# One-hot tiles of the gate matrices laid out token by token, all made on VectorE, with six more score blocks in that stage

## The chip, the cores and the metric

The kernel runs on one core of a Trainium2 chip. The metric is the device time of one execution in microseconds; a smaller number is better. TensorE (PE) multiplies matrices into PSUM, VectorE (DVE), ScalarE (ACT) and GpSimd (POOL) do elementwise work, and SyncE (SP) issues most of the transfers. Every engine works through its own instructions in the order in which they stand, and waits for the others through semaphores.

## What is computed

Two transformer blocks on 512 tokens of width 1024. Each ends in a feed-forward layer of 16384 experts, of which every token takes 16 for each of 8 heads (128 in all). The part of the reference that the change touches, the same in both blocks:

```
s = einsum('thsd,hsnd->thsn', q, sub_keys)      # two halves of 128 keys
sv, si = top_k(s, 16)
cand = sv[:, :, 0, :, None] + sv[:, :, 1, None, :]
top, pos = top_k(cand, 16)                      # 16 experts per head
e = take_along_axis(cidx, pos)                  # expert numbers
g = softmax(top)                                # gates
act = gelu(einsum('thkd,td->thk', u_tab[e], xb))
out = einsum('thk,thkd->td', g * act, v_tab[e])
```

## The kernel before, in words

The function `peer` is called twice, once for each block's expert layer, and takes about half of the span. Its last 128 tokens (tile `TL`) gather their experts' rows from DRAM. For the other 384 tokens (`NDT`) nothing is gathered: the layer is computed densely over all 16384 experts, in 128 blocks of 128 experts. It has these stages.

1. **Routing** (`peer_route`) finds each token's 128 expert numbers `ei` and gates `GT`. Meanwhile PE makes the first 19 **score blocks**. A score block `e` is `gelu(U_e x)` for 128 experts and 384 tokens: a load of `ur`, a rounded part `uh` on ACT, the rest `ul` on POOL, 24 matmuls into `pa`, and a Gelu on ACT into the tile `ga`. At most `NA` = 28 finished blocks lie in SBUF.
2. **The gate stage** builds the dense gate matrix: for each token a 128 x 128 matrix G[e // 128, e % 128] with the gates of its 128 chosen experts. With p running over the token's 128 choices it is a matmul of two one-hot tiles: `oh2` (the low 7 bits of the number equal to the column) and `oh1` (the high 7 bits equal to the column, times the gate; itself the product of the small tiles `oha`, 8 wide, and `ohb`, 16 wide). The stage goes over 12 groups (`NTG`) of 32 tokens (`TG`). For every 8 tokens two instructions over 128 x 1024 elements make `oh2` (on VectorE, line 1199) and `oh1` (line 1201: on GpSimd, and each fourth on VectorE). PE multiplies token by token into `pgg`, four tokens to a PSUM tile, and ACT copies each into `stg` (line 1209). After 32 tokens `stg` goes to DRAM (`Gd`). In the tiles the token index runs fastest, so the 128 elements that PE reads for one token lie 8 elements (32 bytes) apart, in both operands. `run_ahead` puts score blocks between the groups: three ahead of the first group (`TB`), one after each group named in `RG` (3, 6, 9, 11), and two behind the stage, up to 28.
3. **The stream** runs over the 128 blocks. Item `e` reads its gates back (`gbuf`, four items to a load), forms `w` = gates x scores on VectorE, splits it and the rows of V into rounded part and rest (`wh`, `wl`, `vh`, `vl`), emits score block `e + 28`, and adds `w V` into the six PSUM tiles `y` with 18 matmuls. Beside it VectorE handles the gathered rows of the last tile (`urow`, `vrow`, gathered by POOL).

The order on VectorE and GpSimd in the stream is that of the code. Elsewhere a scheduler places instructions by priority, so that a block's matmuls can stand among those of the gate matrices.

Of the kernel before, what the change touches and what calls it, by code (L numbers as in the profile page):

```python
# [23 lines left out]
def build(tc, I, out, dbg=None, stop=None):  # L24
# [571 lines left out]
    for h in range(8):  # L596
# [14 lines left out]
        for t in range(NT):  # L611
# [142 lines left out]
    for h2 in range(2):  # L754
        if h2 == 1:
            ws = keep_w(wk, I["w_mem_o"], 8, 0)
        for t in range(NT):
# [3 lines left out]
            for hh in range(2):  # L761
# [10 lines left out]
                for j in range(2):  # L772
# [298 lines left out]
    def peer(keysT_d, U, UT, Vt, front, finish, nm, side=None, also=None, then=None):  # L1071
# [108 lines left out]
        irep = r1.tile([128, 128, 8], BF16, name="irep")  # L1180
        V.tensor_copy(out=irep, in_=iota.unsqueeze(2).broadcast_to([128, 128, 8]))
        irtg = r1.tile([128, 16, TG], BF16, name="irtg")
        V.tensor_copy(out=irtg, in_=iota[:, 0:16].unsqueeze(2).broadcast_to([128, 16, TG]))
        for tg in range(NTG):
            stg = rw.tile([128, 128, TG], F32, name="stg", tag="stg")

            def row(j, c0, n, m):
                return sT[j][:, c0:c0 + n].unsqueeze(1).broadcast_to([128, m, n])

            c0 = tg * TG  # L1190
            oa_ = rw.tile([128, 8, TG], F32, name="oha", tag="oha")
            V.tensor_tensor(out=oa_, in0=irtg[:, 0:8], in1=row(0, c0, TG, 8), op=OP.is_equal)
            V.tensor_tensor(out=oa_, in0=oa_, in1=row(3, c0, TG, 8), op=OP.mult)
            ob_ = rw.tile([128, 16, TG], F32, name="ohb", tag="ohb")
            V.tensor_tensor(out=ob_, in0=irtg, in1=row(1, c0, TG, 16), op=OP.is_equal)
            for t8 in range(TG // 8):
                tk = slice(t8 * 8, t8 * 8 + 8)
# [6 lines left out]
                for q in range(2):  # L1204
# [668 lines left out]
```

## Time and profile before

| | us |
|---|---|
| median of 3 executions | 4033.55 (4032.31 to 4042.46) |
| the profiled execution | 4039.25, of which the span is 4037.5 |
| PE busy | 3859.8 (96% of the span) |
| DVE busy | 3101.3 (77%) |
| POOL busy | 2146.8 (53%) |
| ACT busy | 1659.2 (41%) |
| mean granted clock of TensorE | 0.977 of full speed |

Shares over the whole span hide that the two expert layers differ from the rest: there one must look at each stage by itself, at which engine has no idle time in it and which engine the others wait for. The gate stage of the first layer runs from 753 to 954 us, that of the second from 2870 to 3070; each is followed by its stream.

### The profile page before, as it was taken

The numbers are of one execution on the slowest core, as the hardware profiler recorded it, in microseconds if no ns is written. First come the engines' busy times: TensorE is split into PE (matmuls) and PEld (weight loads), VectorE is DVE, ScalarE is ACT, GpSimd is POOL, SyncE is SP. The second block draws the span as 40 slices with busy tenths as digits, with TensorE's granted clock in tenths as the row PEclk, the third lists the DMA queues.
The fourth block names the chain that finished last, engine by engine and source line by source line (L and its number), as shares of the span: only waits on it lengthen the run. The fifth ranks groups of instructions, "written<-read, shape, count | busy, mean of one in ns | idle before, by whom it ended". The sixth has DMA issues, their size and how long they took to land. (4 is left out here: it accounts for less than half of the span.)

```text
span 4037.5 us, 53263 instructions
## 1 busy us (share of the span) xinstructions
PE 3859.8 (96%) x19062; PEld 3367.6 (83%) x19062; DVE 3101.3 (77%) x5460; ACT 1659.2 (41%) x2567; POOL 2146.8 (53%) x1333
## 2 busy tenths in 40 slices
PE   6999999899999999999899988999899999999999
PEld 5767788899899999987777766788899999999987
DVE  8456589884898888877756566689885898888875
ACT  3454432454333333333444567332454333333333
POOL 3000047654788887750424433257655778887750
PEclk8999999999999999999999989999999999999999
DMA  3333132235999889987222322332236999999884
GB/s 112 98 102 115 61 112 74 103 133 195 313 332 316 314 315 314 328 286 261 91 81 58 93 73 93 116 111 78 106 136 218 320 324 316 315 317 314 303 272 151
DMA packets 330057, 784.31 MB, mean 194 GB/s; under 512 B 32048, under 2 KB 148864, under 8 KB 326400
## 3 DMA queue, kind: packets, MB, share of 16 engines
q1 hardware_dynamic: 252608, 499.86, 37.6%
q0 software_dynamic: 77184, 281.05, 19.5%
q8 instruction: 150, 2.46, 0.2%
q14 instruction: 115, 0.94, 0.1%
HBM read 722.98 MB, written 56.65 MB: 193 GB/s over the span
## 5 line engine op out<-in xcount | busy, mean ns | idle before, releaser
L1106 POOL TENSOR_TENSOR ul<-ur,uh 128x1024 fp32r<-128x1024 f32 x256 | 713.7, 2788 | 263.9 <-ACT uh L1100 177.1
L1113 PE MATMUL pa<-phi,uh 128*128 128x384 f32 x2048 | 695.1, 339 | 0.6 <-ACT ga L1118 0.6
L1114 PE MATMUL pa<-plo,uh 128*128 128x384 f32 x2048 | 694.2, 339 | 0.0
L1300 PE MATMUL y<-vl,wh 128*128 128x512 f32 x1536 | 599.8, 392 | 5.7 <-DVE vl L1273 5.7
L1301 PE MATMUL y<-vh,wl 128*128 128x512 f32 x1536 | 601.8, 393 | 0.0
L1299 PE MATMUL y<-vh,wh 128*128 128x512 f32 x1536 | 595.6, 392 | 1.7 <-ACT vh L1272 1.6
L1273 DVE TENSOR_TENSOR vl<-vr,vh 128x1024 fp32r<-128x1024 f32 x256 | 341.4, 1334 | 216.1 <-ACT vh L1272 215.9
L1248 DVE SCALAR_TENSOR_TENSOR acc<-vrow,act,acc 128x1024 f32<-128x1024 f32 x256 | 423.6, 1655 | 50.0 <-DMA vrow<-in_expert_v_dram,ei 25.3
L1237 DVE SCALAR_TENSOR_TENSOR urow<-urow,hgat 128x1024 f32<-128x1024 f32 x256 | 416.5, 1634 | 28.9 <-DMA urow<-in_peer_u_dram,ei 17.4
L1271 ACT CAST wh<-w 128x384 fp32r<-128x384 f32 x256 | 131.4, 513 | 745.8 <-PE y L1300 607.0
L1116 PE MATMUL pa<-phi,ul 128*128 128x384 f32 x2048 | 403.9, 340 | 18.5 <-POOL ul L1106 18.4
L1100 ACT CAST uh<-ur 128x1024 fp32r<-128x1024 f32 x256 | 269.6, 1053 | 356.6 <-issue 233.4
L1113 PEld LDWEIGHTS pa<-phi,uh 128*128 128x128 f32 x2048 | 388.7, 190 | 9.8 <-ACT ga L1118 1.0
L1114 PEld LDWEIGHTS pa<-plo,uh 128*128 128x128 f32 x2048 | 388.8, 190 | 9.6
L1116 PEld LDWEIGHTS pa<-phi,ul 128*128 128x128 f32 x2048 | 362.9, 190 | 21.0 <-POOL ul L1106 21.0
L1207 PE MATMUL pgg<-oh,oh 128*128 128x128 f32 x1536 | 373.8, 421 | 4.8 <-DVE oh L1199 4.0
L1207 PEld LDWEIGHTS pgg<-oh,oh 128*128 128x128 f32 x1536 | 369.9, 337 | 7.2 <-issue 5.0
L1301 PEld LDWEIGHTS y<-vh,wl 128*128 128x128 f32 x1536 | 288.7, 188 | 65.8 <-DVE wl L1274 2.7
L1300 PEld LDWEIGHTS y<-vl,wh 128*128 128x128 f32 x1536 | 289.0, 188 | 64.6 <-DVE vl L1273 9.5
L1299 PEld LDWEIGHTS y<-vh,wh 128*128 128x128 f32 x1536 | 288.4, 188 | 57.4 <-ACT vh L1272 4.0
L77 DVE TENSOR_TENSOR wl<-wr,wh 128x512 fp32r<-128x512 f32 (+1 forms) x276 | 201.4, 738 | 146.9 <-ACT wh L76 146.8
L1270 DVE TENSOR_TENSOR w<-gbuf,ga 128x384 f32<-128x384 f32 x256 | 261.8, 1024 | 45.7 <-DMA ur<-in_expert_uT_dram 21.6
(538 smaller groups left out, 7662.9 us busy)
## 6 DMA issues: line engine op xcount, KB each, us to landing
vr<-in_peer_v_dram SPq DMA_DIRECT2D x128, 512.0 KB, 6.2
ur<-in_peer_uT_dram SPq DMA_DIRECT2D x128, 512.0 KB, 4.1
vr<-in_expert_v_dram SPq DMA_DIRECT2D x128, 512.0 KB, 6.7
ur<-in_expert_uT_dram SPq DMA_DIRECT2D x128, 512.0 KB, 4.3
gbuf<-Gd SPq DMA_DIRECT2D x64, 768.0 KB, 9.7
Gd<-stg SPq DMA_DIRECT2D x24, 1920.0 KB, 6.1
wr<-in_w_in_dram SPq DMA_DIRECT2D x104, 256.0 KB, 2.7
war<-in_w_ada_dram SPq DMA_DIRECT2D x24, 512.0 KB, 6.9
```

What stands on the lines that cost most here:

```text
L1100: A.copy(out=uh, in_=ua[e])
L1106: G.tensor_tensor(out=ul, in0=raw, in1=uh.bitcast(F32), op=OP.subtract)
L1113: T.matmul(pa, uh[:, k, :], hi[:, k, 0:NDT], start=(k == 0), stop=False)
L1114: T.matmul(pa, uh[:, k, :], lo[:, k, 0:NDT], start=False, stop=False)
L1116: T.matmul(pa, ul[:, k, :], hi[:, k, 0:NDT], start=False, stop=(k == 7))
L1207: T.matmul(pg[:, j, :], oh2[:, :, 4 * q + j], oh1[:, :, 4 * q + j], start=True, stop=True)
L1237: V.scalar_tensor_tensor(out=row, in0=row, scalar=1.0, in1=hg_, op0=OP.mult, op1=OP.mult, accum_out=act[:, k:k + 1])
L1248: V.scalar_tensor_tensor(out=acc, in0=rows_.pop((1, k)), scalar=act[:, k:k + 1], in1=acc, op0=OP.mult, op1=OP.add)
L1273: V.tensor_tensor(out=vl, in0=vr, in1=vh.bitcast(F32), op=OP.subtract)
L1299: T.matmul(y[t][c], wh[:, ts], vh[:, cs_], start=(e_ == 0), stop=False)
L1300: T.matmul(y[t][c], wh[:, ts], vl[:, cs_], start=False, stop=False)
L1301: T.matmul(y[t][c], wl[:, ts], vh[:, cs_], start=False, stop=(e_ == 127))
```

## The change

The one-hot tiles become token-major: `oh2` and `oh1` are [128, 8 tokens, 128] in place of [128, 128, 8 tokens], so that a token's 128 elements lie side by side. `oha` and `ohb` are turned in the same way. VectorE makes all of them; GpSimd has none left. The constant tiles `irep` and `irtg`, which repeated the column numbers, go; a broadcast view of a 128-wide `iob` takes their place, and the token's value is now the operand that is repeated along the inner dimension. `oh1` has two buffers in place of three.

`run_ahead` now works off a list `todo`: the blocks 19 to 27, and six more, 36, 52, 68, 84, 100 and 116. Three go ahead of the first group, one after each of the 12 groups. The six have no room among the 28 tiles `ga`: they are made in tiles `gs`, written to DRAM (`gad`), and when the stream comes to the item that would have made one (8, 24, 40, 56, 72, 88), a load of 192 KB brings it back in its place.

```
-    O1 = 3
+    TK = 8
+    SP = 16
-        def a_mm(e):
+        def a_mm(e, keep=None):
...
-            ga = ub.tile([128, NDT], F32, name="ga", tag="ga", bufs=NA)
+            ga = keep.tile([128, NDT], F32, name="gs", tag="gs") if keep else ub.tile([128, NDT], F32, name="ga", tag="ga", bufs=NA)
             A.activation(out=ga, in_=pa, func=AF.Gelu)
-            gas[e] = ga
+            if keep:
+                S.dma_start(out=gad[e], in_=ga)
+            else:
+                gas[e] = ga
...
+        gad = {e: dram.tile([128, NDT], F32, name=f"gad{nm}{e}") for e in range(NA + SP // 2, 128, SP)}
+        todo = list(range(16 + TA, NA)) + list(gad)
+        def run_ahead(n, keep):
+            for _ in range(min(n, len(todo))):
+                e = todo.pop(0)
+                emit_A(e, keep if e in gad else None)
...
+        def eq_row(out, n, m, j, c0):
+            V.tensor_tensor(out=out, in0=iob[:, 0:m].unsqueeze(1).broadcast_to([128, n, m]),
+                            in1=sT[j][:, c0:c0 + n].unsqueeze(2).broadcast_to([128, n, m]), op=OP.is_equal)
...
-                oh2 = rw.tile([128, 128, 8], F32, name="oh2", tag="oh2")
-                V.tensor_tensor(out=oh2, in0=irep, in1=row(2, c0 + t8 * 8, 8, 128), op=OP.is_equal)
-                oh1 = rw.tile([128, 128, 8], F32, name="oh1", tag="oh1", bufs=O1)
-                (V if (tg * 4 + t8) % GM == GR else G).tensor_tensor(
-                    out=oh1.rearrange("p (a b) t -> p a b t", a=8), in0=oa_[:, :, tk].unsqueeze(2).broadcast_to([128, 8, 16, 8]),
-                    in1=ob_[:, :, tk].unsqueeze(1).broadcast_to([128, 8, 16, 8]), op=OP.mult)
+                oh2 = rw.tile([128, TK, 128], F32, name="oh2", tag="oh2")
+                eq_row(oh2, TK, 128, 2, c0 + tk)
+                oh1 = rw.tile([128, TK, 128], F32, name="oh1", tag="oh1")
+                V.tensor_tensor(out=oh1.rearrange("p t (a b) -> p t a b", a=8), in0=oa_[:, tk:tk + TK].unsqueeze(3).broadcast_to([128, TK, 8, 16]),
+                                in1=ob_[:, tk:tk + TK].unsqueeze(2).broadcast_to([128, TK, 8, 16]), op=OP.mult)
...
-                        T.matmul(pg[:, j, :], oh2[:, :, 4 * q + j], oh1[:, :, 4 * q + j], start=True, stop=True)
+                        T.matmul(pg[:, j, :], oh2[:, q + j, :], oh1[:, q + j, :], start=True, stop=True)
...
-            if tg in RG:
-                run_ahead(1)
+            run_ahead(-(-len(todo) // (NTG - tg)), gsp)
...
-        run_ahead(NA)
...
-                if e + NA < 128:
+                if e + NA in gad:
+                    gas[e + NA] = ub.tile([128, NDT], F32, name="ga", tag="ga", bufs=NA)
+                    S.dma_start(out=gas[e + NA], in_=gad[e + NA])
+                elif e + NA < 128:
                     emit_A(e + NA)
```

How the order moves. On PE, where the first group of the gate stage begins, the program before has this (`pgg` is the gate matrix of 8 tokens per row, `oh` the one-hot tiles, `pa` a score block):

```order
L1207 MATMUL pgg<-oh_7216,oh_7214 128x128 x8
L1207 MATMUL pgg<-oh_7232,oh_7230 128x128 x8
L1207 MATMUL pgg<-oh_7248,oh_7246 128x128 x8
L1207 MATMUL pgg<-oh_7264,oh_7262 128x128 x8
L1207 MATMUL pgg<-oh_7288,oh_7286 128x128 x8
L1207 MATMUL pgg<-oh_7304,oh_7302 128x128 x8
L1207 MATMUL pgg<-oh_7320,oh_7318 128x128 x8
L1207 MATMUL pgg<-oh_7336,oh_7334 128x128 x8
L1207 MATMUL pgg<-oh_7360,oh_7358 128x128 x8
L1113 MATMUL pa<-phi,uh 128x384
```

In the changed program the same place on PE reads:

```order
L1213 MATMUL pgg<-oh_7223,oh_7221 128x128 x8
L1213 MATMUL pgg<-oh_7239,oh_7237 128x128 x8
L1111 MATMUL pa<-phi,uh 128x384
L1112 MATMUL pa<-plo,uh 128x384
L1111 MATMUL pa<-phi,uh 128x384
L1112 MATMUL pa<-plo,uh 128x384
L1213 MATMUL pgg<-oh_7255,oh_7253 128x128 x8
L1111 MATMUL pa<-phi,uh 128x384
L1112 MATMUL pa<-plo,uh 128x384
L1111 MATMUL pa<-phi,uh 128x384
L1213 MATMUL pgg<-oh_7271,oh_7269 128x128 x8
```

Each group's 32 tokens now share the queue with one score block, of which 4 matmuls stand behind 16 tokens, 3 behind 24 and 17 behind all 32. After the last group 17 + 48 matmuls of score blocks stand ahead of the first `y`, where there were 96 before, and the first two items' `y` (36 matmuls) follow each other without a block between them.

On VectorE, in the second group of the stage, the program before has one row of two for each 8 tokens (the `oh1` of three rows in four is on GpSimd):

```order
L1192 TENSOR_TENSOR oha<-irtg,sT_7074 128x256
L1199 TENSOR_TENSOR oh_7286<-irep,sT_7076 128x1024
L1193 TENSOR_TENSOR oha<-oha,sT_7077 128x256
L1195 TENSOR_TENSOR ohb<-irtg,sT_7075 128x512
L1199 TENSOR_TENSOR oh_7302<-irep,sT_7076 128x1024
L1199 TENSOR_TENSOR oh_7318<-irep,sT_7076 128x1024
L1201 TENSOR_TENSOR oh_7336<-oha,ohb 128x1024
L1199 TENSOR_TENSOR oh_7334<-irep,sT_7076 128x1024
```

In the changed program VectorE's rows of one group (from the middle of the second into the third) are:

```order
L1193 TENSOR_TENSOR oha<-iob,sT_7080 128x256
L1193 TENSOR_TENSOR ohb<-iob,sT_7081 128x512
L1201 TENSOR_TENSOR oha<-oha,sT_7083 128x256
L1193 TENSOR_TENSOR oh_7358<-iob,sT_7082 128x1024
L1208 TENSOR_TENSOR oh_7360<-oha,ohb 128x1024
L1193 TENSOR_TENSOR oh_7374<-iob,sT_7082 128x1024
L1208 TENSOR_TENSOR oh_7376<-oha,ohb 128x1024
L1193 TENSOR_TENSOR oh_7431<-iob,sT_7082 128x1024
L1208 TENSOR_TENSOR oh_7433<-oha,ohb 128x1024
L1193 TENSOR_TENSOR oh_7447<-iob,sT_7082 128x1024
L1208 TENSOR_TENSOR oh_7449<-oha,ohb 128x1024
```

So a group takes three small instructions and eight of 1024 elements on VectorE, where it took three small ones and five large ones.

## Rows read from the trace of the kernel before

**Rows 1.** Windows: gate stage, stream's start, streams. Stretch, length, busy time (instructions) by engine, clock, DMA.
```profile
753.00:954.00 201.00, 198.19 (x841) 197.02 (x841) 151.95 (x89) 102.98 (x102) 116.60 (x40) 0.99 0.32 129
...
971.00:1100.00 129.00, 127.95 (x639) 114.39 (x639) 97.14 (x114) 47.20 (x67) 83.76 (x52) 1.00 0.87 292
1100.00:1700.00 600.00, 598.89 (x3031) 544.57 (x3030) 542.86 (x510) 218.37 (x295) 484.52 (x262) 1.00 0.91 320
3200.00:3800.00 600.00, 600.00 (x3043) 546.31 (x3042) 538.47 (x509) 219.75 (x297) 484.86 (x262) 1.00 0.91 318
```

**Rows 2.** One line's instructions in the first gate stage: ns min/median/max, first and last start.
```profile
L1207 PE MATMUL pgg<-oh,oh x768: 415/420/578, 752.8 to 953.7; 128*128 128x128 f32 x192
```

**Rows 3.** Timeline of PE: start us, us, line, instruction, count; gate matrices, routing scores; the latter's ns min/median/max.
```profile
802.64 15.67 PE L1207 MATMUL pgg<-oh,oh 128*128 128x128 f32 x64
...
2792.13 1.05 PE L910 MATMUL psc<-keysT,qs 128*128 128x128 f32 x8
...
L910 PE MATMUL psc<-keysT,qs x256: 270/275/377, 539.4 to 2817.0; 128*128 128x128 f32 x128
```

**Rows 4.** Timeline of PE around one score block: its first matmul, the `y` behind it.
```profile
975.21 0.34 PE L1113 MATMUL pa<-phi,uh 128*128 128x384 f32 x1
...
979.38 0.39 PE L1299 MATMUL y<-vh,wh 128*128 128x512 f32 x1
```

**Rows 5.** Single lines of VectorE over the whole span: ns min/median/max.
```profile
L1192 DVE TENSOR_TENSOR oha<-irtg,sT x24: 417/2572/2622, 743.0 to 3029.4; 128x256 f32<-128x256 bf16 x24
...
L1195 DVE TENSOR_TENSOR ohb<-irtg,sT x24: 677/679/2871, 743.4 to 3031.9; 128x512 f32<-128x512 bf16 x24
...
L1199 DVE TENSOR_TENSOR oh<-irep,sT x96: 1211/1226/3423, 744.3 to 3062.6; 128x1024 f32<-128x1024 bf16 x96
...
L1201 DVE TENSOR_TENSOR oh<-oha,ohb x24: 1216/1218/3400, 760.1 to 3059.9; 128x1024 f32<-128x1024 f32 x24
...
L966 DVE TENSOR_TENSOR ec<-eq,cidx x4: 983/988/1606, 725.1 to 2848.4; 128x800 f32<-128x800 bf16 x4
```

**Rows 6.** Timeline of DVE in the gate stage: two large instructions in a row.
```profile
774.95 1.23 DVE L1199 TENSOR_TENSOR oh<-irep,sT 128x1024 f32<-128x1024 bf16 x1 [0.33 <-PE pgg L1207]
776.09 1.22 DVE L1201 TENSOR_TENSOR oh<-oha,ohb 128x1024 f32<-128x1024 f32 x1
```

**Rows 7.** Timeline of POOL and DVE side by side, and the line of the score blocks' rest on POOL.
```profile
798.82 2.59 POOL L1201 TENSOR_TENSOR oh<-oha,ohb 128x1024 f32<-128x1024 f32 x1 [0.51 <-PE pgg L1207]
799.11 3.38 DVE L1199 TENSOR_TENSOR oh<-irep,sT 128x1024 f32<-128x1024 bf16 x1
...
L1106 POOL TENSOR_TENSOR ul<-ur,uh x256: 2337/2628/3386, 538.9 to 3897.7; 128x1024 fp32r<-128x1024 f32 x128
```

**Rows 8.** The copy of four tokens' gates from PSUM on ACT.
```profile
L1209 ACT COPY stg<-pgg x192: 1012/1022/1132, 755.0 to 3070.3; 128x512 f32<-128x512 f32 x192
```

**Rows 9.** Timeline behind the last gate matmul: copy, store, load of gates, `w`, first `y`.
```profile
954.16 1.10 ACT L1209 COPY stg<-pgg 128x512 f32<-128x512 f32 x1 [0.91 <-PE pgg L1207]
...
955.66 0.42 SPq L1211 DMA_DIRECT2D Gd<-stg  x1
...
962.66 0.55 SPq L1262 DMA_DIRECT2D gbuf<-Gd  x1
...
969.20 0.56 DVE L1270 TENSOR_TENSOR w<-gbuf,ga 128x384 f32<-128x384 f32 x1 [21.48 <-POOL ul L1106]
...
970.62 0.39 PE L1299 MATMUL y<-vh,wh 128*128 128x512 f32 x1
```

**Rows 10.** Timeline of PE at a gap in the gate stage, and two windows of PE alone.
```profile
2883.05 2.25 PE L1207 MATMUL pgg<-oh,oh 128*128 128x128 f32 x8 [1.62 <-DVE oh L1199]
...
2883.70:2887.10 3.40, 3.40 (x16) 0.50 0.00 0
2391.00:2402.00 11.00, 7.46 (x35) 0.81 0.44 131
```

**Rows 11.** Waits in the first stream (1100 to 1700): us in total, times, longest.
```profile
ACT wh L1271 <- PE y L1300: 235.9, 69, 3.5
```

More of the change, by code (lines that the diff above doesn't have):

```diff
@@ L848, in build @@
     EW = 120
-    GM = 4
-    GR = 3
     TB = 3
+    TK = 8
+    SP = 16
     NA = 28
@@ L1054, in build @@
     EB = 4
-    RG = (3, 6, 9, 11)
     DVE_ = mybir.EngineType.DVE
@@ L1116, in a_mm, with emit_A @@
                 T.matmul(pa, ul[:, k, :], hi[:, k, 0:NDT], start=False, stop=(k == 7))
-            ga = ub.tile([128, NDT], F32, name="ga", tag="ga", bufs=NA)
+            ga = keep.tile([128, NDT], F32, name="gs", tag="gs") if keep else ub.tile([128, NDT], F32, name="ga", tag="ga", bufs=NA)
             A.activation(out=ga, in_=pa, func=AF.Gelu)
-            gas[e] = ga
-        def emit_A(e):
+            if keep:
+                S.dma_start(out=gad[e], in_=ga)
+            else:
+                gas[e] = ga
+        def emit_A(e, keep=None):
             a_dma(e)
@@ L1124, in emit_A @@
             a_lo(e)
-            a_mm(e)
+            a_mm(e, keep)
         gas = {}
@@ L1133, in load_v @@
             return vr
-        def run_ahead(n):
-            for e in range(len(gas), min(NA, len(gas) + n)):
-                emit_A(e)
+        gad = {e: dram.tile([128, NDT], F32, name=f"gad{nm}{e}") for e in range(NA + SP // 2, 128, SP)}
[4 more added lines that the diff above has]
+                emit_A(e, keep if e in gad else None)
         E = rr.tile([128, 4, 128], F32, name="E")
@@ L1177, in peer @@
         ix.close()
-        run_ahead(TB)
+        gsp = rp.enter_context(tc.tile_pool(name=nm + "gs", bufs=2))
+        run_ahead(TB, gsp)
         rw = rp.enter_context(tc.tile_pool(name=nm + "gg", bufs=2))
[L1180 to L1183, printed above, removed]
+        iob = r1.tile([128, 128], BF16, name="iob")
@@ L1184, in peer @@
+        V.tensor_copy(out=iob, in_=iota)
+        def eq_row(out, n, m, j, c0):
+            V.tensor_tensor(out=out, in0=iob[:, 0:m].unsqueeze(1).broadcast_to([128, n, m]),
+                            in1=sT[j][:, c0:c0 + n].unsqueeze(2).broadcast_to([128, n, m]), op=OP.is_equal)
         for tg in range(NTG):
             stg = rw.tile([128, 128, TG], F32, name="stg", tag="stg")
-            def row(j, c0, n, m):
-                return sT[j][:, c0:c0 + n].unsqueeze(1).broadcast_to([128, m, n])
@@ L1190, in peer @@
             c0 = tg * TG
[L1191 to L1197, printed above, removed]
-                oh2 = rw.tile([128, 128, 8], F32, name="oh2", tag="oh2")
-                V.tensor_tensor(out=oh2, in0=irep, in1=row(2, c0 + t8 * 8, 8, 128), op=OP.is_equal)
-                oh1 = rw.tile([128, 128, 8], F32, name="oh1", tag="oh1", bufs=O1)
-                (V if (tg * 4 + t8) % GM == GR else G).tensor_tensor(
-                    out=oh1.rearrange("p (a b) t -> p a b t", a=8), in0=oa_[:, :, tk].unsqueeze(2).broadcast_to([128, 8, 16, 8]),
-                    in1=ob_[:, :, tk].unsqueeze(1).broadcast_to([128, 8, 16, 8]), op=OP.mult)
-                for q in range(2):
+            oa_ = rw.tile([128, TG, 8], F32, name="oha", tag="oha")
@@ new lines, in peer @@
+            eq_row(oa_, TG, 8, 0, c0)
+            V.tensor_tensor(out=oa_, in0=oa_, in1=sT[3][:, c0:c0 + TG].unsqueeze(2).broadcast_to([128, TG, 8]), op=OP.mult)
+            ob_ = rw.tile([128, TG, 16], F32, name="ohb", tag="ohb")
+            eq_row(ob_, TG, 16, 1, c0)
+            for tk in range(0, TG, TK):
+                oh2 = rw.tile([128, TK, 128], F32, name="oh2", tag="oh2")
[3 more added lines that the diff above has]
+                                in1=ob_[:, tk:tk + TK].unsqueeze(2).broadcast_to([128, TK, 8, 16]), op=OP.mult)
+                for q in range(0, TK, 4):
@@ L1205, in peer @@
                     pg = psm.tile([128, 4, 128], F32, name="pgg", tag="mm")
                     for j in range(4):
-                        T.matmul(pg[:, j, :], oh2[:, :, 4 * q + j], oh1[:, :, 4 * q + j], start=True, stop=True)
-                    ts = t8 * 8 + 4 * q
-                    A.copy(out=stg[:, :, ts:ts + 4].rearrange("p e t -> p t e"), in_=pg)
+                        T.matmul(pg[:, j, :], oh2[:, q + j, :], oh1[:, q + j, :], start=True, stop=True)
+                    A.copy(out=stg[:, :, tk + q:tk + q + 4].rearrange("p e t -> p t e"), in_=pg)
```

## The prediction

> **What bounds the kernel now.** I read the windows first. In the gate stage PE is busy 198.2 of 201 us, and in both streams 598.9 and 600.0 of 600; VectorE has 152 us in the stage and about 540 in each stream stretch [rows 1]. So PE sets the time in every stage that the change touches, and what counts is PE's time and any new gap on it. The second view is PE's timeline, to turn durations into steps, since matmuls overlap. A gate matmul (one token) leaves two records, hence 768 for 384 tokens [rows 2]. 64 records take 15.67 us [rows 3]; less the 0.42 of the last one [rows 2], over 63, that is **0.242 us a record**. The routing scores have the same shape, 128 x 128 f32, but operands whose elements lie side by side: 8 records take 1.05 us, one alone 0.275 [rows 3], so the step is 0.775 / 7 = **0.111**. A score block of 24 matmuls moves the next `y` back by 979.38 - 975.21 = **4.17 us** [rows 4].
>
> **Gate matmuls.** What is changed for PE is only that the 128 elements of a token, 32 bytes apart before, are adjacent. By the nearest row a record falls from 0.242 to 0.111 us, 768 x 0.131 = 101 us of PE time in each layer. This could all be had only if the others kept up, so next I look at them.
>
> **One group of 32 tokens after the change.** PE: 64 x 0.111 + 4.17 for the one block = 11.3 us. VectorE: a large instruction takes 1.21 to 1.23 us alone, and two in a row start 1.14 us apart [rows 6]; eight are 9.1. The two 256-wide ones take 0.42 and the 512-wide one 0.68 [rows 5]; with the same overlap of 0.08 that is 0.34 + 0.34 + 0.60 = 1.3. Sum 10.4. The new layout repeats the token's value along the inner dimension. A row that does this already, L966, takes 0.983 us for 800 elements where L1199 takes 1.211 for 1024 [rows 5]: 1.23 and 1.18 ns an element, the difference being the fixed part, so I add nothing. POOL loses its one-hot work but still makes the block's `ul`. VectorE waits out a POOL instruction whole: 3.38 us in place of 1.2 beside one that ended 2.3 us after it began [rows 7]. So `ul` adds about 2.4 (its shortest is 2.34 [rows 7]): **12.8 us a group**, more than PE's 11.3. ACT has 8 copies of 1.02 = 8.2 [rows 8] and the block's two instructions, below both. VectorE therefore becomes the bound of the stage, by 1.5 us a group, and PE waits for it.
>
> **Length of the stage.** VectorE begins at 743.0 [rows 5]. The `ul` of the first block falls ahead of it, so 12 x 10.4 + 11 x 2.4 = 151. At the start it fills its two pairs of tiles and stands until PE, busy with the three blocks ahead, takes the first at 752.8 [rows 2]; laid out step by step that costs some 5 us, and `ul` of the blocks ahead about 2. The last pair's matmuls (16 x 0.111) and the last copy add 3 to 4: 743 + 151 + 5 + 2 + 4 = **905** for the end of the last copy, where it was 955.3 [rows 9]. Gain 50.3 us.
>
> **Behind the stage.** Before, the chain copy, store (955.66), load of gates (962.66), `w` (969.20), first `y` (970.62) took 15.4 us after the copy [rows 9], just covered by 96 matmuls of blocks. Nothing in this chain is changed, so `y` starts near 920.4. But only 17 + 48 matmuls remain to cover it, 65 x 4.17 / 24 = 11.3 us; PE is idle some 4 us. A gap of 1.62 us in the second gate stage was followed by 3.4 us at a granted clock of 0.50, the 1.2 GHz level [rows 10]; at half speed 3.4 us do the work of 1.7, and I charge 2 us.
>
> **The six blocks.** At the first `y` there were 19 + 3 + 4 + 2 + 1 = 29 blocks done; now 19 + 15 + 2 = 36. The stream is bound by PE, so these 7 are worth 7 x 4.17 = 29.2 us there. Where a block is missing, two items' `y` stand together and PE asks for the next weights 4.17 us sooner. What hides this is that the weights are a full item ahead: in 600 us, with 72 items, ACT's cast of `w` waited 69 times for PE to give back a buffer [rows 11], and VectorE has 10% idle to catch up over 16 items [rows 1]. Only at the stream's start is that lead not built up (PE 127.95 of 129, though VectorE has only 97 [rows 1]); there stand the first pair and the one at item 8. If that cover is gone each costs up to 4.17. I take 5 us in the first layer and 2 in the second. The loads of `gad` (192 KB for 512 KB of `ur`) make traffic less; each waits on SP's queue for the `w` that frees its tile, with a load of V behind it, six times, which the same lead covers. The six stores are 192 KB each in a stage with a DMA share of 0.32 [rows 1]; nothing waits for them for many items. Dropping `irep` and `irtg` lies beside routing's end and PE's blocks ahead; I take nothing.
>
> **Sum.** 50.3 + 29.2 - 2 - 3.5 = 74 us for a layer, 148 for both. The profiled execution took 4039.25, 5.7 more than the median; 4039.25 - 148 = 3891, on the scale of the median **3886 us**.
>
> **Bounds.** (1) VectorE's step: 1.14, or 1.22 if no two overlap, 8 x 0.08 x 12 = 8 us a layer dearer. (2) `ul`: 2.4, or 0 if it runs while VectorE waits for a tile; then PE's 11.3 sets the group and 1.5 x 12 = 18 us a layer are won. (3) The record: 0.111 to 0.242; up to 0.13 VectorE hides it (64 x 0.13 + 4.17 = 12.5), the far end is rival C. (4) Clock: while PE was busy 7.5 of 11 us, in the second block's attention, the granted clock was 0.81 [rows 10]; 11.3 / 0.81 = 13.9, over VectorE's 12.8 by 1.1, 13 us a layer. (5) Stream: 0 to all six pairs exposed, 25 us; I allow 8 more than the sum has. Together 3886 - 36 - 7 = 3843 at the low end, and 3886 + 2 x (8 + 13 + 8) = 3944 at the high end.
>
> **Rivals.**
> A. *PE stays the bound* (bound 2, with nothing lost in the stream): 3886 - 43 = 3843 to 3865. For it: VectorE stands for a tile in each group while the block's last 17 matmuls run. Against: `ul` follows ACT's cast, which stands behind the group's copies, so it starts just when VectorE could go on. Chance 0.15.
> B. *The clock gives way*, or several pairs are exposed in the stream: 3912 to 3944. For it: the gap in rows 10 was hardly longer than the waits foreseen, 12.8 - 11.3 = 1.5 us once a group. Against: a fall that costs PE 1.7 us uses up those 1.5 first. Chance 0.14. [...]
> C. *The record doesn't get shorter*: the 0.242 us have another cause than the spacing. Then a group is 64 x 0.242 + 4.17 = 19.7 us of PE, 12 of them 236 from 752.8 on; the last copy ends at 990, 35 us later than before; 35 - 29.2 + 2 + 3.5 = 11 us a layer, **4056**, slower. It decides from a record of 0.228 us on (11 / 768 less). For it: no row shows this matmul in another layout. Against: the routing scores, same shape and engine, at 0.111 [rows 3]. From this row alone, chance 0.04. The Trainium skill (SBUF — State Buffer, Door 1: The DMA port swizzle) names the spacing as a cause: reads that stay within one 16-byte line run at full bandwidth, each step to a new line pays. By that rule every element of the old layout pays and C falls away; by the rows, which hold two different matmuls, it stays possible, and I leave it its 0.04.
> D. *VectorE's instructions are dearer in the new layout*: at 1.5 us a step 96 x 0.36 = 35 us a layer, 3955; all is lost at 1.14 + 74 / 96 = 1.91. Against it L966. Chance 0.05, a third of that beyond 1.8.
>
> **How the numbers follow.** Forecast 0.62, A 0.15, B 0.14, C 0.04, D 0.05. The likeliest gives 3886. The range 3843 to 3944 holds the forecast, A and nearly all of B. A measurement tells 0.3% (12 us) from no change; faster by more: 0.94; within it 0.02 (D near its point, C with a small gain); slower 0.04 (C, and D's far end).
>
> **What would show it.** In the changed profile: a gate record's step at 0.11 (else C); large VectorE instructions of 1.22 us with 1.14 steps, a few of 3.4 us beside `ul`; the first `y` 50 us earlier after the stage's start; the gate matmuls waiting for VectorE's tiles once a group; a gap of about 4 us ahead of the first `y`; PE without gaps in the stream but at its start. The prediction is wrong if VectorE's instructions are longer alone, if PE shows a clock below 0.95 in the stage, or if PE waits at the pairs later in the stream.

## The result, and the profile after

The changed kernel takes 3875.97 us (median of 4 runs, 3871.71 to 3882.67), beside 4032.93 us (4029.94 to 4042.46, 4 runs) for the kernel before: ratio 0.9608, 95% interval 0.9586 to 0.9631, a gain of 157 us. The prediction was 3886 us and a gain of 148.

The profiled execution took 3871.71 us (span 3870.0), 4.3 less than its median, as that of before took 5.7 more than its own. So the two traces differ by 167.5 us, of which some 10 are scatter between executions. Where they lie, in us, each from the start or end of the instruction named:

| stretch | before, layer 1 / 2 | after, layer 1 / 2 | change |
|---|---|---|---|
| VectorE's first small tile to the first gate matmul | 9.8 / 10.6 | 10.2 / 10.5 | +0.4 / -0.1 |
| first gate matmul to the end of the last copy to `stg` | 202.4 / 201.7 | 150.1 / 150.0 | -52.3 / -51.7 |
| last copy to the first `y` | 15.4 / 15.4 | 16.6 / 17.3 | +1.2 / +1.9 |
| first `y` to the last `y` | 962.9 / 942.1 | 932.7 / 914.3 | -30.2 / -27.8 |
| all before layer 1; between the layers | 743.0; 925.7 | 737.3; 922.3 | -5.7; -3.4 |

The last line holds little of the change: two casts on VectorE that made `irep` and `irtg` (0.68 and 0.42 us) give way to one of 0.22. They are not the cause of the 5.7 and 3.4 us, for the first matmul of the routing scores, far ahead of these casts, already starts 5.1 and 3.8 us earlier. In the twelve experiments below the first number lies between 737.3 and 744.3 and the second between 916.9 and 935.7, so I take this as scatter.

The windows answer to [rows 1]: the gate stage, the way to the first `y`, and two stretches of the stream. Columns: stretch, length, busy time (instructions) of PE, weight loads, VectorE, ScalarE and GpSimd, granted clock, DMA share, GB/s.

```profile
750.00:890.00 140.00, 131.25 (x974) 125.17 (x973) 137.59 (x121) 105.68 (x111) 27.11 (x12) 1.00 0.55 209
897.00:915.00 18.00, 11.51 (x64) 11.10 (x63) 4.40 (x3) 7.15 (x9) 11.14 (x8) 0.94 0.93 317
915.00:1044.00 129.00, 127.86 (x629) 114.45 (x628) 98.10 (x120) 48.09 (x67) 80.12 (x50) 0.98 0.88 297
1044.00:1644.00 600.00, 600.00 (x3028) 544.61 (x3027) 532.27 (x524) 218.39 (x295) 478.29 (x263) 1.00 0.93 326
```

In the stage VectorE is now the busiest engine, 137.59 of 140 us, and PE has 8.75 us idle where it had 2.8 of 201. In the stream PE is as full as before. The gate matmuls themselves, ns min/median/max, answer to [rows 2]:

```profile
L1213 PEld LDWEIGHTS pgg<-oh,oh x768: 186/192/192, 747.3 to 896.1; 128*128 128x128 f32 x192
L1213 PE MATMUL pgg<-oh,oh x768: 272/275/377, 747.5 to 896.2; 128*128 128x128 f32 x192
```

A record alone is 0.275 us, as that of the routing scores [rows 3]. Sixteen of them in a row take 1.95 us (PE, start and length; the bracket is the wait ahead of the row and what ended it):

```profile
785.94 1.95 PE L1213 MATMUL pgg<-oh,oh 128*128 128x128 f32 x16
788.17 2.06 PE L1213 MATMUL pgg<-oh,oh 128*128 128x128 f32 x16 [0.29 <-ACT stg L1214]
...
791.38 2.02 PE L1213 MATMUL pgg<-oh,oh 128*128 128x128 f32 x16 [0.44 <-ACT stg L1214]
```

(1.95 - 0.275) / 15 = 0.112 us a step. The short waits are put down to ScalarE's copy, which is not what bounds the stage; the runs with six tiles and with one more comparison show that below. VectorE's own timeline beside GpSimd's answers to [rows 6] and [rows 7]:

```profile
785.44 0.42 DVE L1193 TENSOR_TENSOR oha<-iob,sT 128x256 f32<-128x256 bf16 x1
...
810.72 0.41 DVE L1193 TENSOR_TENSOR oha<-iob,sT 128x256 f32<-128x256 bf16 x1
811.06 0.68 DVE L1193 TENSOR_TENSOR ohb<-iob,sT 128x512 f32<-128x512 bf16 x1
811.52 2.45 POOL L1104 TENSOR_TENSOR ul<-ur,uh 128x1024 fp32r<-128x1024 f32 x1 [10.19 <-PE pa L1114]
811.66 2.59 DVE L1201 TENSOR_TENSOR oha<-oha,sT 128x256 f32<-128x256 f32 x1
814.17 1.21 DVE L1193 TENSOR_TENSOR oh<-iob,sT 128x1024 f32<-128x1024 bf16 x1
815.31 1.21 DVE L1208 TENSOR_TENSOR oh<-oha,ohb 128x1024 f32<-128x1024 f32 x1
```

Two groups lie between the first two rows, so a group takes (810.72 - 785.44) / 2 = 12.64 us. The large instructions keep their length in the new layout (1.21) and their step (815.31 - 814.17 = 1.14). The small multiply, 0.42 us where nothing is beside it, begins 0.14 us after GpSimd's `ul` and takes 2.59: 2.17 us of a group are spent waiting out `ul`. It takes 2.58 to 2.63 in 23 of the 24 groups.

Behind the stage (copy, score blocks, stores and loads, `w`, `y`; this answers to [rows 9]):

```profile
895.58 2.02 ACT L1214 COPY stg<-pgg 128x512 f32<-128x512 f32 x2 [0.35 <-PE pgg L1213]
898.00 0.42 SPq L1216 DMA_DIRECT2D Gd<-stg  x1
904.22 2.00 SPq L1265 DMA_DIRECT2D gbuf<-Gd  x2
906.18 1.55 PE L1114 MATMUL pa<-phi,ul 128*128 128x384 f32 x8
910.60 3.02 DVE L1273 TENSOR_TENSOR w<-gbuf,ga 128x384 f32<-128x384 f32 x1 [16.40 <-DMA gbuf<-Gd]
910.85 2.35 POOL L1104 TENSOR_TENSOR ul<-ur,uh 128x1024 fp32r<-128x1024 f32 x1
914.22 1.65 PE L1305 MATMUL y<-vh,wh 128*128 128x512 f32 x3 [6.49 <-ACT wh L1274]
...
925.07 0.34 PE L1111 MATMUL pa<-phi,uh 128*128 128x384 f32 x1
...
912.80:919.60 6.80, 5.38 (x13) 0.50 0.99 378
```

PE has finished its blocks at 907.7 and waits 6.49 us. `w` takes 3.02 us where it took 0.56; a `ul` on GpSimd runs beside it and ends 0.4 us ahead of it. The 36 `y` matmuls up to 925.07 take 10.85 us. The last row is a window of PE alone: length, busy time, granted clock, DMA share, GB/s.

### The profile page after: what moved, and what is told of

The parts are those of the page before. It is cut to its first block, busy times and chain, and to the rows that moved or that the text cites. A ratio compares the mean times of both kernels' runs of the same rounds, so it can differ in the third digit from the quotient of the medians.

```text
span 3870.0 us, 53220 instructions
## 1 busy us (share of the span) xinstructions
PE 3667.4 (95%) x19062; PEld 3166.8 (82%) x19062; DVE 3028.6 (78%) x5530; ACT 1654.5 (43%) x2567; POOL 1915.2 (49%) x1261
## 3 DMA queue, kind: packets, MB, share of 16 engines
q0 software_dynamic: 77184, 281.05, 20.3%
## 5 line engine op out<-in xcount | busy, mean ns | idle before, releaser
L1104 POOL TENSOR_TENSOR ul<-ur,uh 128x1024 fp32r<-128x1024 f32 x256 | 696.3, 2720 | 436.6 <-PE pa L1114 251.5
L1276 DVE TENSOR_TENSOR vl<-vr,vh 128x1024 fp32r<-128x1024 f32 x256 | 359.5, 1404 | 210.6 <-ACT vh L1275 182.6
L1251 DVE SCALAR_TENSOR_TENSOR acc<-vrow,act,acc 128x1024 f32<-128x1024 f32 x256 | 408.4, 1595 | 56.5 <-DMA vrow<-in_peer_v_dram,ei 28.4
L1240 DVE SCALAR_TENSOR_TENSOR urow<-urow,hgat 128x1024 f32<-128x1024 f32 x256 | 407.6, 1599 | 29.2 <-DMA urow<-in_peer_u_dram,ei 17.2
L1111 PEld LDWEIGHTS pa<-phi,uh 128*128 128x128 f32 x2048 | 389.3, 190 | 10.2 <-ACT ga L1116 1.9
L1275 ACT CAST vh<-vr 128x1024 fp32r<-128x1024 f32 x256 | 267.7, 1046 | 33.2 <-DMA vr<-in_peer_v_dram 16.0
L1273 DVE TENSOR_TENSOR w<-gbuf,ga 128x384 f32<-128x384 f32 x256 | 214.7, 841 | 38.0 <-issue 18.7
L76 ACT CAST wh<-wr 128x512 fp32r<-128x512 f32 (+1 forms) x276 | 149.2, 551 | 200.1 <-PE mm L120 125.9
```

The costliest lines, as they stand in the source:

```text
L1104: G.tensor_tensor(out=ul, in0=raw, in1=uh.bitcast(F32), op=OP.subtract)
L1240: V.scalar_tensor_tensor(out=row, in0=row, scalar=1.0, in1=hg_, op0=OP.mult, op1=OP.mult, accum_out=act[:, k:k + 1])
L1251: V.scalar_tensor_tensor(out=acc, in0=rows_.pop((1, k)), scalar=act[:, k:k + 1], in1=acc, op0=OP.mult, op1=OP.add)
L1275: A.copy(out=vh, in_=vr)
L1276: V.tensor_tensor(out=vl, in0=vr, in1=vh.bitcast(F32), op=OP.subtract)
```

## The experiments

The theory of the prediction, here V: with the elements side by side a gate record steps by 0.111 us, and VectorE bounds the stage with 10.4 us of its own in a group and some 2.4 of waiting for GpSimd (2.17 in the trace above). L is that the layout makes most of the gain by itself. Rivals and open questions: W, that each of the two spaced operands makes the record long by itself; P, that PE and ScalarE, passing two PSUM tiles to and fro, set the pace of the stage. In the tables below "stage" is the time from the first gate matmul to the end of the last copy, layer 1 / layer 2.

### One part alone

**The layout without the six blocks.** The changed kernel with the blocks placed as before:

```
-        gad = {e: dram.tile(...) for e in range(NA + SP // 2, 128, SP)}
+        gad = {}
-            run_ahead(-(-len(todo) // (NTG - tg)), gsp)
+            if tg in (3, 6, 9, 11):
+                run_ahead(1, gsp)
...
+        run_ahead(NA, None)
```

> Changed layout and VectorE alone, with the score blocks as before: 4 between the groups, 2 behind the stage, none in DRAM. Theory L (the gain is the shorter gate record; the six blocks only fill PE's waits in a stage that VectorE bounds): gate record 0.111 us, stage (first gate matmul to last copy) 12 x 10.4 + 4 x 2.4 and 3 to 5 at its ends = 138 us or a little less, against 150 with the six blocks and 202 before; the first y some 14 us earlier than with them but 7 blocks (29 us) poorer, so 11 to 15 us a layer slower than the whole change: 3898 to 3906. Rival F (the filling with blocks is the larger half of the gain): 3950 or more.

3902.55 us, ratio 0.967 (0.9643 to 0.9697); stage 142.7 / 145.3, where 138 was expected. The total came as expected, though not by the expected way: the scheduler pulled all the blocks into the stage (192 `pa` matmuls there, none behind it; the kernel before had 72 and 96), and PE, with nothing left to do, waited from the last gate matmul on:

```profile
907.92 0.79 PE L1307 MATMUL y<-vh,wh 128*128 128x512 f32 x1 [15.23 <-ACT wh L1276]
```

So the layout with the move to VectorE brings some 130 of the 157 us. No run has the new layout with GpSimd's share of `oh1` left to it, so how the 130 divide between the two is not shown. What the blocks add on top is about 27 us: six in each layer that the stream need not make, a tail with cover, less a longer stage.

**The six blocks without the layout.** The kernel before with `todo`, `gad` and the loads of the change, and its own one-hot tiles:

```
+        todo = list(range(16 + TA, NA)) + list(gad)
...
-            if tg in RG:
-                run_ahead(1)
+            run_ahead(-(-len(todo) // (NTG - tg)), gsp)
...
-        run_ahead(NA)
```

> The kernel before with the six more blocks and their way through DRAM, old layout and engines. Theory L: PE bounds the stage and the stream, so blocks only move: stage longer by 8 x 4.17 = 33 us, stream shorter by 29, and a shorter cover behind the stage: 4033 to 4050. Rival F: the six blocks gain by themselves, 20 to 60 us: 3975 to 4013.

4053.62 us, ratio 1.0038 (1.0024 to 1.0053): slower by about 15 us, just beyond what L expected. The profiled execution took 4069.19. The stage grows to 234.3 / 233.7, the streams shrink to 938.3 / 916.2. In a stage that PE bounds, a block costs PE there what it saves later; and the tail has lost its cover. Layer 1's first `y` in this kernel:

```profile
1006.30 1.65 PE L1309 MATMUL y<-vh,wh 128*128 128x512 f32 x3 [6.48 <-ACT wh L1278]
```

The same 6.5 us as in the changed kernel: that gap belongs to the moving of the blocks, not to the new layout. Moving these blocks pays only together with the layout.

**All of `oh1` on VectorE, in the old layout.**

```
-    GM = 4
-    GR = 3
+    GM = 1
+    GR = 0
```

> The kernel before with every oh1 on VectorE (none on GpSimd), old layout, blocks as before. Theory L: PE stays the bound of the stage with 64 x 0.242 = 15.5 us a group against VectorE's 10.4 to 12.8: within 6 us of 4033. Rival: sharing the tiles with GpSimd is what holds the stage up (VectorE's instructions of 3.4 us go): 20 us or more faster.

4061.71 us, ratio 1.0061 (1.0045 to 1.0078): 25 us more than before, a miss. In the stage nothing is wrong; PE is simply full (columns as in the windows above), and the record's step is 0.240 as before:

```profile
760.00:960.00 200.00, 200.00 (x876) 199.25 (x876) 124.64 (x116) 99.36 (x100) 21.69 (x7) 1.00 0.33 131
...
976.90:993.90 17.00, 4.98 (x11) 3.71 (x12) 5.17 (x8) 5.29 (x8) 4.11 (x5) 0.50 0.98 321
```

The loss is behind it. With faster one-hot tiles the scheduler put 189 of the blocks' 192 matmuls into the stage, so that 3 were left to cover the chain to the first `y`:

```profile
988.92 0.79 PE L1299 MATMUL y<-vh,wh 128*128 128x512 f32 x1 [14.99 <-ACT wh L1271]
```

Some 15 us of PE idle a layer, and 5 us of `y` at half clock after it. The expectation held the engine to be the only thing the edit changes; it also changed the order. In the stage the move is worth little: 117 matmuls of blocks more, at 4.17 / 24 us each, are 20.3 us, and it grew by 18.3, from 202.4 to 220.7. As long as PE bounds the stage, who makes the tiles hardly counts.

### Which operand makes the record long

The changed kernel, VectorE and blocks as in it, with one of the two one-hot tiles in the old layout. First `oh1`, the moving operand (with `oha` and `ohb`, of which it is made):

```
-                oh1 = rw.tile([128, TK, 128], F32, name="oh1", tag="oh1")
+                oh1 = rw.tile([128, 128, TK], F32, name="oh1", tag="oh1")
...
-                        T.matmul(pg[:, j, :], oh2[:, q + j, :], oh1[:, q + j, :], start=True, stop=True)
+                        T.matmul(pg[:, j, :], oh2[:, q + j, :], oh1[:, :, q + j], start=True, stop=True)
```

> The changed kernel, but oh1 (the moving operand) again with its 128 elements 32 bytes apart; oh2 (the weights) stays side by side. If either spacing alone makes the record long: 0.242 us, group 19.7, stage 236 us, about 4048. If the weights' spacing is what costs: 0.111, 3876. If the moving operand alone does part of it, between.

4030.7 us, ratio 0.9987 (0.9973 to 1.0002); stage 227.8 / 227.8, shorter than the 236 expected, since the step is 0.233 us and not 0.242. Then `oh2`, the weights:

```
-                oh2 = rw.tile([128, TK, 128], F32, name="oh2", tag="oh2")
+                oh2 = rw.tile([128, 128, TK], F32, name="oh2", tag="oh2")
...
-                        T.matmul(pg[:, j, :], oh2[:, q + j, :], oh1[:, q + j, :], start=True, stop=True)
+                        T.matmul(pg[:, j, :], oh2[:, :, q + j], oh1[:, q + j, :], start=True, stop=True)
```

> The changed kernel, but oh2 (the weights) again with its 128 elements 32 bytes apart; oh1 (moving) side by side. The run with the moving operand spaced gave a record of 0.233 us. Theory W (each operand's read is slowed by its own spacing, and the slower read sets the step): 0.23 to 0.24 us a record, stage 228 us, about 4031. Theory M (only the moving operand's spacing counts, the load of weights hides beside it): 0.111, 3876.

4037.39 us, ratio 1.001 (0.9993 to 1.0027); stage 229.4 / 229.2; a step of 0.234 us. The gate matmuls of the first layer, all of them and some in a row, moving operand spaced:

```profile
L1218 PEld LDWEIGHTS pgg<-oh,oh x768: 186/208/209, 751.5 to 977.6; 128*128 128x128 f32 x192
L1218 PE MATMUL pgg<-oh,oh x768: 390/412/447, 751.6 to 977.8; 128*128 128x128 f32 x192
...
808.97 7.63 PE L1218 MATMUL pgg<-oh,oh 128*128 128x128 f32 x32
```

and with the weights spaced:

```profile
L1218 PEld LDWEIGHTS pgg<-oh,oh x768: 312/335/336, 749.8 to 977.5; 128*128 128x128 f32 x192
L1218 PE MATMUL pgg<-oh,oh x768: 328/402/473, 749.8 to 977.6; 128*128 128x128 f32 x192
...
800.95 3.91 PE L1218 MATMUL pgg<-oh,oh 128*128 128x128 f32 x16
```

The steps are (7.63 - 0.41) / 31 = 0.233 and (3.91 - 0.40) / 15 = 0.234 us. Theory W: either operand alone makes the record long. A spaced moving operand lengthens the matmul (275 to 412 ns, the load hardly: 208); spaced weights lengthen the load (192 to 335 ns) and the matmul's record with it (402), and the step comes out the same. With both spaced it is 0.242 [rows 3], or 0.240 in the run with all of `oh1` on VectorE: the two prices don't add. With half of the layout change the whole is no faster than the kernel before.

### What bounds the new stage

**One comparison more on VectorE in each group.**

```
                 eq_row(oh2, TK, 128, 2, c0 + tk)
+                if tk == 0:
+                    eq_row(oh2, TK, 128, 2, c0 + tk)
```

> The changed kernel with one comparison of a group (oh2, 1.21 us) made twice: VectorE's work grows by 1.21 us in each of 12 groups, nothing else changes. Theory V: the stage grows by all of it, 13 to 15 us a layer, to 163 to 165, and the whole time by 26 to 30, to 3902 to 3906. Theory P: the stage stays at 150 to 154 and the whole within 8 us of the changed kernel. Both together: 5 to 11 us a layer.

3900.08 us, ratio 0.9675 (0.9658 to 0.9691), 24 us more than the changed kernel; stage 162.7 / 161.2, that is 12.6 / 11.2 longer. VectorE's timeline:

```profile
801.79 2.36 DVE L1193 TENSOR_TENSOR oh<-iob,sT 128x1024 f32<-128x1024 bf16 x2
...
805.19 2.59 DVE L1193 TENSOR_TENSOR oha<-iob,sT 128x256 f32<-128x256 bf16 x1
...
818.88 2.58 DVE L1193 TENSOR_TENSOR oha<-iob,sT 128x256 f32<-128x256 bf16 x1
```

A group is 818.88 - 805.19 = 13.69 us, 1.05 longer for an instruction whose step is 1.14 (2.36 for the pair, less 1.22). All groups behind the stage's start took 13.66 to 13.70. The stage grew by a little less than expected because the instruction costs its step in a row and not the 1.21 us that it takes alone. Nearly all of what is put on VectorE appears in the time: V.

**Six PSUM tiles in place of two.**

```
+                    pool, tag = ((psm, "mm"), (pst, "tr"), (pss, "sc"))[(tk + q) // 4 % 3]
-                    pg = psm.tile([128, 4, 128], F32, name="pgg", tag="mm")
+                    pg = pool.tile([128, 4, 128], F32, name="pgg", tag=tag)
```

> The changed kernel with its pgg tiles taken in turn from three PSUM pools, so six tiles instead of two stand between TensorE and ScalarE's copies; order and VectorE's work are the same. Theory V (VectorE is the bound of the stage, 98% busy in the profiled run): the stage from the first pgg to the last copy stays at 149 to 151 us a layer, the group at 12.5 to 12.7, 3870 to 3882 in all. Theory P (the round trip of TensorE and ScalarE through two tiles, 2.29 us for 8 tokens in the VectorE-light run, is the bound): the group falls to TensorE's own 11.3 to 11.5, the stage to 136 to 140, 3846 to 3856 in all. Both together (VectorE waits now and then for TensorE to give back a one-hot tile): 144 to 148, 3862 to 3870.

3877.86 us, ratio 0.9605 (0.9588 to 0.9623); stage 149.6 / 149.1: no gain, as V expected. Windows of 760 to 880 us and two rows of PE, a group apart:

```profile
760.00:880.00 120.00, 110.72 (x842) 107.96 (x842) 120.00 (x107) 90.25 (x96) 22.55 (x10) 1.00 0.54 207
...
809.18 2.02 PE L1214 MATMUL pgg<-oh,oh 128*128 128x128 f32 x16 [1.03 <-DVE oh L1208]
...
821.79 2.02 PE L1214 MATMUL pgg<-oh,oh 128*128 128x128 f32 x16 [1.03 <-DVE oh L1208]
```

VectorE has not a moment idle, the group is 12.61 us, and PE's wait now stands under VectorE's name. In the changed kernel the same idle time was split into small waits of which most were booked on ScalarE, since its copy gave the last of two events.

**A quarter of the `oh1` instructions.**

```
-                oh1 = rw.tile([128, TK, 128], F32, name="oh1", tag="oh1")
-                V.tensor_tensor(out=oh1.rearrange(...), ...)
+                if tk == 0:
+                    oh1 = rw.tile([128, TK, 128], F32, name="oh1", tag="oh1")
+                    V.tensor_tensor(out=oh1.rearrange(...), ...)
```

> The changed kernel with oh1 made once for each 32 tokens and used for all four sets of 8 (this leaves out three of four products, so the gates are partly those of other tokens): VectorE has 3.4 us less in a group. Theory V: VectorE falls to 9.2 us, below PE's 11.3, and the stage becomes PE's: 136 to 142 us in place of 150, 3848 to 3860 in all. Rival P: the stage stays at 150 us, 3876.

3890.89 us, ratio 0.9653 (0.9629 to 0.9676); stage 156.6 / 155.4, **longer** by 6, with three VectorE instructions fewer in each group. What theory V expected did not come. VectorE is busy only 72.61 of 120 us, but with the tiles early the scheduler put all 64 records of a group in a row and the whole block behind them (PE, then ScalarE):

```profile
760.00:880.00 120.00, 113.40 (x818) 108.09 (x817) 72.61 (x72) 87.94 (x93) 21.20 (x9) 1.00 0.53 203
...
806.44 2.05 PE L1214 MATMUL pgg<-oh,oh 128*128 128x128 f32 x16 [0.29 <-ACT stg L1215]
808.73 2.08 PE L1214 MATMUL pgg<-oh,oh 128*128 128x128 f32 x16 [0.24 <-ACT stg L1215]
...
807.63 1.96 ACT L1215 COPY stg<-pgg 128x512 f32<-128x512 f32 x2 [0.36 <-PE pgg L1214]
```

Eight tokens take 808.73 - 806.44 = 2.29 us, where PE's 16 records want 16 x 0.112 = 1.79: two copies of 1.96 us together and 0.33 of waiting for PE, in turn. So P is a bound too: three times 2.29 and 1.87 for the last eight tokens' records are 8.7 us, and with the block's 4.2 behind them a group is 12.9. In the changed kernel the block's matmuls between the records cover part of that, and VectorE's 12.64 hides the rest.

**The rest `ul` of the stage's blocks by VectorE.**

```
-            run_ahead(-(-len(todo) // (NTG - tg)), gsp)
+            run_ahead(-(-len(todo) // (NTG - tg)), gsp, V)
...
-            G.tensor_tensor(out=ul, in0=raw, in1=uh.bitcast(F32), op=OP.subtract)
+            eng.tensor_tensor(out=ul, in0=raw, in1=uh.bitcast(F32), op=OP.subtract)
```

> The changed kernel, but in the gate stage VectorE makes the 12 blocks' ul itself (1.14 us) where GpSimd did and VectorE waited out its 2.4 us. Theory V (VectorE bounds the stage): a group takes 10.4 + 1.14 = 11.5 in place of 12.6 us, 11 to 14 us a layer less, 3848 to 3854. Rival P (the copies from PSUM, for which PE's waits are booked, bound it: PE needs ACT's two PSUM tiles back): the group stays at 12.6, 3876.

3863.64 us, ratio 0.9582 (0.9556 to 0.9608); stage 142.9 / 142.8. VectorE does more, and the stage is 7.2 us shorter in each layer: what GpSimd took off VectorE, 1.14 us a group, had cost it 2.17 of waiting. But only half of the expected gain came, and the group stood at 12.1 us with VectorE at 11.54 by its own steps (8 x 1.14 for the large ones, 1.14 for `ul`, 1.28 for the small). The next run tells why.

**Both: `ul` on VectorE and six PSUM tiles.** The edits of the two runs above together.

> The ul of the stage's blocks by VectorE (as in the run with the rest on VectorE) and six pgg tiles. That run had stage 142.9, group 12.05, and neither TensorE (116.9 of 120) nor VectorE (115.9 of 120) left more than 4 us idle. Theory P for that run (its last 0.5 us a group were the round trip through two PSUM tiles): the group comes to the larger of TensorE's 11.4 and VectorE's 11.65, the stage to 137 to 140, 3852 to 3859 in all. Theory V for it (VectorE was the bound there too): stage 142 to 144, 3861 to 3867.

3854.09 us, ratio 0.9558 (0.9538 to 0.9578); stage 137.2 / 137.1. The windows of 760 to 880 us, first with two tiles and `ul` on VectorE:

```profile
760.00:880.00 120.00, 116.91 (x877) 113.65 (x877) 115.88 (x120) 95.16 (x100) 0.00 (x0) 1.00 0.60 226
...
DVE oh L1193 <- PE pgg L1213: 4.1, 10, 0.5
```

(the last row is a wait: us in total, times, longest), then with six:

```profile
760.00:880.00 120.00, 120.00 (x916) 117.70 (x916) 120.00 (x125) 98.54 (x105) 0.00 (x0) 1.00 0.61 226
...
810.95 0.42 DVE L1193 TENSOR_TENSOR oha<-iob,sT 128x256 f32<-128x256 bf16 x1
...
822.51 0.42 DVE L1193 TENSOR_TENSOR oha<-iob,sT 128x256 f32<-128x256 bf16 x1
```

VectorE's waits for PE, some 0.4 us a group, are gone, the group is 11.56, and PE and VectorE are both full. So the round trip through two tiles was what held the run before it: the same edit that brought nothing while VectorE needed 12.64 us brings 5.7 us a layer once VectorE needs 11.54.

### The cover behind the stage

**The first group's block put behind the stage**, which leaves 88 in place of 65 matmuls behind the last gate record:

```
-            run_ahead(-(-len(todo) // (NTG - tg)), gsp)
+            if tg:
+                run_ahead(1, gsp)
+        run_ahead(NA, gsp)
```

> The changed kernel with the first group's block left out and one more block behind the stage, so that PE has 65 + 24 matmuls (15.5 us) ahead of the first y, where it stood idle 6.5 us. If VectorE bounds the stage, a ul less makes it 2.4 us shorter, the first y comes 2.4 us sooner and the clock does not fall behind it (2 to 3 us): 8 to 11 us less in all, 3865 to 3868. Rival (the gap ahead of the first y costs nothing, since the chain through DRAM sets the first y): 4 to 5 us less at most, 3871 to 3876.

3872.04 us, ratio 0.9607 (0.9585 to 0.9629). The first `y` of the two layers:

```profile
910.79 0.96 PE L1307 MATMUL y<-vh,wh 128*128 128x512 f32 x3 [1.44 <-ACT wh L1276]
...
2949.78 0.96 PE L1307 MATMUL y<-vh,wh 128*128 128x512 f32 x3 [2.85 <-ACT wh L1276]
```

PE's idle time ahead of it falls from 6.5 / 7.3 to 1.4 / 2.9 us and the time at half clock from 6.8 / 6.8 to 0 / 3.4; the stage is 2.6 / 3.1 shorter. Yet the expected 3865 to 3868 did not come, and the total is within the scatter of the changed kernel's: layer 1's stream was some 5 us longer in this trace. No more than that can be said of it.

**The same edit on top of both.**

> As the run with both, and the first group's block moved behind the stage, so that 3.7 blocks instead of 2.7 stand between the last gate record and the first product of the stream. A block less in the stage saves VectorE 1.2 us and TensorE 4.2 us of one group (1 to 4 us a layer), a block more behind it hides 4.2 us of TensorE's idle time there and 3 us at half clock. If the stream keeps its length: 3 to 8 us below the run with both, 3845 to 3853. If the time only moves into the stream, as the run with one block behind showed: within 4 us of the run with both.

3840.93 us (median of 5, 3838.91 to 3854.89), ratio 0.9532 (0.9513 to 0.955); stage 132.4 / 132.3. It lies below the 3845 to 3853 expected, and is the fastest version of the study, 35 us below the changed kernel and some 190 below the one before.

```profile
760.00:880.00 120.00, 119.95 (x928) 117.51 (x927) 119.84 (x125) 98.65 (x107) 0.00 (x0) 1.00 0.62 235
...
895.11 0.45 PE L1111 MATMUL pa<-phi,uh 128*128 128x384 f32 x1 [2.05 <-ACT uh L1098]
```

PE is idle 2.1 / 1.9 us here, within the blocks behind the stage, with 3.4 us at a granted clock of 0.50 after it; the first `y` follows the blocks without a wait. Of the step from the run with both, the traces explain 4.8 us a layer in the stage and 0.5 behind it, less 3.1 / 2.4 of longer streams: about 5 in all. The medians differ by 13 and the intervals of the two overlap, so the rest lies in the scatter and is left open.

## Why the prediction was right, point by point

- **The gate record, 0.242 to 0.111.** Held: 0.112. The row of the routing scores [rows 3] was a sound stand-in, and rival C with its 4% didn't come. The Trainium skill (SBUF — State Buffer, Door 1: The DMA port swizzle) has every read that steps to another 16-byte line pay; the runs agree that spacing is the cause, 0.233 us with one operand spaced against 0.112, and show something it doesn't say, that one spaced operand costs nearly as much as two. No run tried another spacing, so where the price begins is not shown.
- **The group, 12.8 us by VectorE.** Held: 12.64. Its own part was 12.64 - 2.17 = 10.47 for 10.4, the wait for `ul` 2.17 for 2.4. That `ul` always falls where VectorE could go on, the argument against rival A, held in 23 of the 24 groups. That VectorE and not PE or ScalarE is the bound, which the waits in the profile alone don't show, is shown by the two runs with a comparison more and with six tiles.
- **The stage's length.** From VectorE's first tile to the last copy 162 was predicted, 160.3 came.
- **Behind the stage.** "Nothing in this chain is changed" was the wrong step: from the last copy to the first `y` it took 16.6 / 17.3 us in place of 15.4. In layer 1 `w` now meets a `ul` on GpSimd (3.02 for 0.56 us), which `w` makes good in part by beginning 0.9 us sooner after the copy; in layer 2 `w` takes 1.53 and begins 15.2 us after the copy, where it was 14.0. The idle time of PE, 4 us predicted, was 6.5 / 7.3: the cover of 11.3 us was set against the 15.4 from the copy's end, when PE's last gate matmul starts 1.4 us ahead of that. The clock was charged at 2 us: PE waited from 907.7 to 914.2, and the granted clock stood at 0.5, the 1.2 GHz level, from 912.8 to 919.6. The 36 `y` took 10.85 us, where at 0.23 each, the step of the rows after, they would take 8.3: 2.6 us. The Trainium skill (TensorE: Matmul & The Clock Gate, Why this matters for your kernels) warns of long idle gaps between bursts of matmuls, behind which the clock falls; the trace agrees for this gap of 6.5 us. The waits of the stage, up to 0.5 us after one of 1.01 at its start, left the clock at 1.00, as did one of 1.03 in every group (six tiles). So the falling clock of rival B did not come, nor, by the next point, its exposed pairs.
- **The six blocks.** 29.2 us a layer less 5 and 2 for the doubled `y` was predicted; the streams are 30.2 / 27.8 shorter, the slow first `y` included. The 7 blocks were worth what was said: 92 stand in the stream in place of 99, at 4.17 us each in both kernels. The charge for the doubled `y` was too high: none of the six later pairs has a gap (their 36 `y` take 8.37 us), and up to the last block PE's gaps are one of 1.14 us in layer 1 and one of 0.24 in layer 2, neither at a pair. The lead of the weights did cover them, at item 8 too.
- **The sum.** 74 us a layer predicted; 52.3 - 1.2 + 30.2 = 81 and 51.7 - 1.9 + 27.8 = 78 in the traces. No term missed by more than 8 us; the largest is layer 1's stream, forecast at 22 us shorter. In the seven kernels with the changed kernel's order of blocks in the stream and behind the stage this stretch lies between 931.3 and 941.1 us, so part of the 8 is scatter. The misses behind the stage and in the stream go opposite ways; that they cancel in part is luck.

Two things the prediction had no word for: two PSUM tiles are a second bound close to VectorE's, at 12.1 to 12.9 us a group by where the block's matmuls stand; and the order is not fixed. The scheduler moved blocks into the stage, or within it, in three runs in which only one-hot instructions or the list of blocks had been edited, and that decided the time of two.

## What to carry to other kernels

When a matmul's step is twice that of the same shape elsewhere in the program, look at the spacing of both operands and mend both; then find the next engine by the sum of its own steps and its waits for GpSimd, and prove it by adding a known piece of work to it, since the name in a short wait can be the wrong one. An instruction given to GpSimd to relieve VectorE may cost VectorE more than making it itself: here 2.17 us of waiting against 1.14. Loosen bounds together where two lie close: more PSUM tiles alone brought nothing, and 5.7 us a layer once VectorE had been relieved.

## What the runs showed of the hardware that was not expected

- One spaced operand, moving or weights, costs the whole price (0.233, 0.234 us a record) and the second hardly any more (0.240 to 0.242). Spaced weights show in the load, 335 in place of 192 ns, and in the matmul, 402 in place of 275; a spaced moving operand shows in the matmul, 412, and hardly in the load, 208.
- In the runs with a gap of 15 us ahead of the first `y` the granted clock was 0.50 for 17 us, some 12 of them inside the gap; with 6.4 to 7.3 us it was 6.8, or 10.2 in four of the layers. What stood behind the gap at the 1.2 GHz level was 3 to 6 us of `y` in either case.
- A gap need not be that long: the one of 1.62 us [rows 10], one of 1.99 at the stage's start in the run with one comparison more, and the 2.05 in the fastest version were each followed by 3.4 us at 0.50, while the 1.44 ahead of the first `y` with one block behind was not.
- The copies on ScalarE took 1.05 to 1.18 us (median 1.093) where they took 1.022 [rows 8], though tile and output stayed the same. No run looked for the cause.
